# Mixer 0: the last strip's split between the first score tables, the rms root by tables, another order of the stick-breaking blocks; mixer 1: GpSimd's scaling later

## The chip, the core and the metric

The kernel runs on one core of a Trainium2 chip. The metric is the device time of one execution in microseconds; below, "us". Engines are named as in the profile: PE (TensorE), DVE (VectorE), ACT (ScalarE), POOL (GpSimd), SP (SyncE, which issues most transfers).

## The reference, cut to what matters

```python
x = LayerNorm(alpha * x + even_mixer(x))      # mixer 0: Mamba-2 SSD heads || stick-breaking heads
x = LayerNorm(alpha * x + hier_moe_0(x))
x = LayerNorm(alpha * x + odd_mixer(x))       # mixer 1: latent attention || forgetting attention
x = LayerNorm(alpha * x + hier_moe_1(x))

def _rms_norm(x, g):
    return x * rsqrt(mean(x * x, -1) + RMS_EPS) * g

# even mixer, its end
y = _ssd_scan(xs, dt, a, bs, cs) + d_skip * xs
y = _rms_norm(y * silu(z), norm_g)
# stick-breaking, per head, 256 tokens, s < t
z = q @ k.T * scale
later = reversed cumulative sum of log_sigmoid(-z) over s, without its own term
sb = where(s < t, exp(log_sigmoid(z) + later), 0) @ v
return concat([y, sb]) @ w_out

# odd mixer, both kinds of heads, per head
prob = softmax(masked logits)                 # forgetting heads add sums of log f
out = prob @ v
return concat([mla, fox]) @ w_out
```

x is [256, 1024], all values are fp32. There are 16 SSD heads and 8 stick-breaking heads of 64 in layer 0, 8 and 8 heads of 64 in layer 1.

## The kernel before, in words

Every fp32 matrix product is made of three products of two pieces: `split` (L225 to L234) takes a weight strip of 128 x 1024, copies its high piece on ACT (L232) and subtracts to get the low piece on DVE (L233). Weights come in transfers of 1 MB, in the order in which they are used, into a ring of 19 slots. There is no scheduler: every engine executes its instructions in the order in which the Python code writes them, and the code interleaves the stages by hand.

**Mixer 0.** The input projection runs through 32 strips; `presplit(i + 2)` splits two strips ahead of the strip that PE multiplies. From strip 20 on, a list `side` holds pieces of the sequence part (the SSD blocks `ssd_m` and `ssd_y`, then `sb_scores(0)` and `ssd_y(7)`), and after each strip `run_side` takes so many of them as the table `RS` says. Strips 28 to 31 are the attention's values (`v_strip`, products at L316). Behind them comes `out_proj`: 12 chunks k of the output weights, for each the three products L731, L732, L733 for two token tiles and two halves. `before(k)` runs ahead of chunk k what `PLAN0` says: `s` is `sb_scores` of a pair of heads (products L527 and L530, a mask by L293, on ACT the tables Abs, Exp, Ln at L536 to L538, on DVE L539 and the pieces L544, L545), `w` is `sb_weights` (L552, L553, the table at L555), `o` is `sb_out` (L564, L565, L566, L567), `r` is `rms` (L666), which sums squares and finds the root with shifts and Newton steps on DVE (`rsqrt_dve`, L769). The first chunks are the SSD output y (`y_scale`, L513 on ACT and L514 on DVE); the root is only applied at chunk 7. PSUM has two pools of four banks, A and B; `self.B("z")` takes the next bank of pool B and waits for its last reader.

**Mixer 1.** PE multiplies strips in the order of the list `order`: first values (`v`, L316, with norms, the turning of the latent pieces L1521 and L1522, key positions in `key_rope` and the forget gates in `forget` between them), then `q`, `kv`, and the eight strips `s`, into which the attention of the first pairs is placed (`attention(i)`): scores with row maxima on DVE (L1601, L1602) and the exponential on ACT (L1605), `norm_probs` (L1611, then L1614 and L1615, two heads each), and the split of the next strip behind them. `forget_rows` makes the rows of summed forget gates that PE multiplies at L1596. `norms` uses `rsqrt_refine` (L217 to L223). GpSimd multiplies the residual by the layer norm's gain (L836) and adds its bias (L837) in `gain_rows`, 256 columns at a time: token tile 0 inside `key_rope`, ahead of the rope's own small operations, and tile 1 in the strips s 0 and s 1. `softplus_small` (L190 to L215) is a chain of small GpSimd operations for the forget gates.

Of the kernel before, what the change touches and what calls it, by code (L numbers as in the profile page):

```python
# [41 lines left out]
for _n, _w in [("ident", 128), ("triU", 128), ("ntriSL", 128), ("sbT", 128),  # L42
# [11 lines left out]

PLAN0 = {0: [("s", 1)], 2: [("w", 0), ("w", 1)], 3: [("r", 0), ("o", 0), ("s", 2)], 4: [("o", 1)],
         5: [("s", 3)], 6: [("w", 2)], 7: [("o", 2)], 8: [("w", 3)], 9: [("o", 3)]}

# [37 lines left out]
class Builder:  # L95
# [224 lines left out]
    def mixer0(self):  # L320
# [198 lines left out]

        def sb_scores(p):  # L520
            if not p:
# [12 lines left out]
            for i, t in enumerate(ts):  # L534
                a = self.T([128, 384], name="spz")
                sc.activation(a, t[:, :384], AF.Abs)  # L536
                sc.activation(a, a, AF.Exp, scale=-1.0)
                sc.activation(a, a, AF.Ln, bias=1.0)  # L538
                v.scalar_tensor_tensor(a, t[:, :384], 0.0, a, op0=OP.max, op1=OP.add)  # L539
                Z[2 * p + i] = (t, a)  # L540
            for i in range(2):
                t, a = Z[2 * p + i]
                hi, lo = (u[:, 2 * (p % 2) + i] for u in sph)
                v.tensor_copy(hi, a)  # L544
                v.tensor_sub(lo, a, hi.bitcast(F32))  # L545
                Z[2 * p + i] = (t, a, hi, lo)
# [31 lines left out]
        for i in range(32):  # L578
# [53 lines left out]
            if i == 20:  # L632
# [4 lines left out]
                for j in range(8):  # L637
                    side += [(ssd_m, (2 * j,)), (ssd_m, (2 * j + 1,))]
                    if j:
                        side.append((ssd_y, (j - 1,)))  # L640
                side += [(sb_scores, (0,)), (ssd_y, (7,))]
            if i == 30:
# [20 lines left out]
        nc.gpsimd.dma_start(self.xres, self.a["x"])  # L663
        rr = self.S([128, 2, 8], name="rr")

        def rms(_):  # L666
            sp = self.B("ssp")
            for t in range(2):
                pe.matmul(sp[:, t:t + 1], ssq[:, 128 * t:128 * t + 128], self.one, start=True, stop=True)
            for t in range(2):  # L670
                v.tensor_scalar(rr[:, t, 1:2], sp[:, t:t + 1], 1.0 / 1024.0, RMS_EPS, op0=OP.mult, op1=OP.add)
                self.rsqrt_dve(rr[:, t, 0:1], rr[:, t, 1:2], rr[:, t, 2:])

# [15 lines left out]
        def between(k, a, t):  # L689
            if k == 7:  # L690
                sc.activation(a, a, AF.Copy, scale=rr[:, t, 0:1])

# [74 lines left out]


    def rsqrt_dve(self, y, x, t):  # L769


        v = self.nc.vector
        yi = y.bitcast(I32)
        v.tensor_scalar(yi, x.bitcast(I32), 1, None, op0=OP.arith_shift_right)
        v.tensor_scalar(yi, yi, -1.0, 1597463007.0 - 3 * 2.0 ** 23 - 2.0 ** 31, op0=OP.mult, op1=OP.add)
        for k, f in enumerate((64.0, 16.0, 4.0)):
            v.tensor_scalar(t[:, k:k + 1], x, f, None, op0=OP.mult)
        for k in range(3):
            v.scalar_tensor_tensor(t[:, 3:4], y, y, t[:, k:k + 1], op0=OP.mult, op1=OP.mult)
            v.scalar_tensor_tensor(y, t[:, 3:4], -3.0, y, op0=OP.add, op1=OP.mult)  # L780

# [603 lines left out]
    def mixer1(self, s0, moe):  # L1385
# [100 lines left out]
        def key_rope():  # L1486
            nc.gpsimd.memset(krep[:, :, :64], 0.0)
            gb.append(self.ln_rows(s0 + 4))
            for k in range(4):
                self.gain_rows(0, gb[0], slice(256 * k, 256 * k + 256))  # L1490
            self.rope(nc.gpsimd, krep[:, :, 64:80], krep[:, :, 80:96], rest[:, :, 128:144], rest[:, :, 144:160],
# [18 lines left out]
        def forget_rows():  # L1510
            fr = A["fr"]
            lp = self.B("lp")
            pe.matmul(lp[:, :128], fr[:, 0, :], self.cv("ntriSL"), start=True, stop=True)
# [147 lines left out]
        for n in range(len(order)):  # L1661
# [39 lines left out]
            if c == "s":  # L1701
                if i < 2:
                    for k in (2 * i, 2 * i + 1):
                        self.gain_rows(1, gb[0], slice(256 * k, 256 * k + 256))
                if i == 7:
# [152 lines left out]
```

## Time and profile before

| | us |
|---|---|
| median of 3 runs | 504.05 |
| lowest, highest run | 504.04, 505.17 |
| the profiled execution, its own time | 505.15 |
| its span on the profile | 503.4 |

| engine | busy us | share of the span | instructions |
|---|---|---|---|
| PE | 486.5 | 97% | 3805 |
| DVE | 301.6 | 60% | 698 |
| ACT | 246.7 | 49% | 512 |
| POOL | 74.6 | 15% | 121 |

The profile records when each instruction began and how long it took, and ends an engine's idle time with the instruction that released it. Its times below count from the start of the span. The profiled execution took 505.15, 1.1 above the median of the runs. PE's granted clock averaged 0.995 of full speed over the span.

### The profile page before, as it was taken

To read this page: it belongs to the slowest core of one execution; us is meant where nothing else is said; L and a number is where in the kernel's file an instruction comes from. 1 tells how busy PE (TensorE), PEld (TensorE's weight loads), DVE (VectorE), ACT (ScalarE), POOL (GpSimd) and SP (SyncE) were. 2 spreads that over 40 slices of the span, in tenths; PEclk is the share of its full clock that TensorE was granted. 3 is DMA by queue.
4 is the path that set the end of the run, shared out by engine and by line. 5 is a ranking of instruction groups with operands and counts; after the bars stand their busy time and mean duration, and the time that the engine had idled before them with its cause. 6 is when DMAs were issued, how large, how long until landed. Compare 5 with 4: busy or idle time off the path is not lost. (4 is left out here: it accounts for less than half of the span.)

```text
span 503.4 us, 9615 instructions
## 1 busy us (share of the span) xinstructions
PE 486.5 (97%) x3805; PEld 315.5 (63%) x3805; DVE 301.6 (60%) x698; ACT 246.7 (49%) x512; POOL 74.6 (15%) x121
## 2 busy tenths in 40 slices
PE   8999999998999999999999999999999999999992
PEld 4999998886867634352333589988777442523330
DVE  4868957767966875152305786788677761411136
ACT  3788576667774434160303667556644351612031
POOL 0074000110000000070000097400000000520003
PEclk9999999999999999999999999999999999999998
DMA  8999952005348969999999792370578799999932
GB/s 313 419 421 416 422 204 85 0 1 201 135 133 332 417 241 425 419 423 420 421 418 415 300 421 103 154 251 1 169 250 317 292 423 422 422 420 421 416 133 83
DMA packets 21313, 146.97 MB, mean 292 GB/s; under 512 B 2385, under 2 KB 2641, under 8 KB 4113
## 3 DMA queue, kind: packets, MB, share of 16 engines
q1 hardware_dynamic: 20016, 140.16, 69.2%
q0 software_dynamic: 816, 5.51, 2.9%
q8 instruction: 31, 0.51, 0.4%
q10 hardware_dynamic: 432, 0.66, 0.4%
q14 instruction: 18, 0.14, 0.1%
HBM read 145.26 MB, written 1.05 MB: 291 GB/s over the span
## 5 line engine op out<-in xcount | busy, mean ns | idle before, releaser
L1095 PE MATMUL gu<-w,XT 128*32 128x512 f32 x960 | 106.5, 593 | 0.4 <-PEq L1320 0.4
L233 DVE TENSOR_TENSOR pair<-w,pair 128x1024 fp32r<-128x1024 f32 x58 | 71.1, 1230 | 17.2 <-ACT pair L232 16.6
L1095 PEld LDWEIGHTS gu<-w,XT 128*32 128x32 f32 x960 | 30.9, 110 | 67.0 <-issue 64.5
L232 ACT ACTIVATE pair<-w 128x1024 fp32r<-128x1024 f32 x58 | 61.3, 1059 | 7.4 <-PE qu L1542 2.8
L1125 PE MATMUL dn<-w,hT 128*32 128x512 f32 x512 | 57.4, 594 | 0.0
L1105 DVE TENSOR_TENSOR hd<-sg,gu 128x256 f32<-128x256 f32 x16 | 6.7, 420 | 69.1 <-ACT sg L1103 69.0
L1148 DVE SCALAR_TENSOR_TENSOR pair<-dn,ws,pair 128x512 fp32r<-128x512 f32 x28 | 21.0, 751 | 41.0 <-ACT pair L1142 39.1
L1103 ACT ACTIVATE sg<-gu 128x256 f32<-128x256 f32 x16 | 6.2, 385 | 78.4 <-PE gu L1095 78.3
L241 PE MATMUL ps<-xh,pair 128*128 128x256 f32 x288 | 41.5, 287 | 0.3 <-ACT pair L374 0.3
L244 PE MATMUL ps<-xl,pair 128*128 128x256 f32 x288 | 39.1, 278 | 0.0
L247 PE MATMUL ps<-xh,pair 128*128 128x256 f32 x288 | 39.0, 278 | 0.0
L241 PEld LDWEIGHTS ps<-xh,pair 128*128 128x128 f32 x288 | 36.1, 189 | 2.1 <-ACT pair L374 0.8
L1125 PEld LDWEIGHTS dn<-w,hT 128*32 128x32 f32 x512 | 15.4, 110 | 33.8 <-issue 29.8
L244 PEld LDWEIGHTS ps<-xl,pair 128*128 128x128 f32 x288 | 35.8, 188 | 0.0
L247 PEld LDWEIGHTS ps<-xh,pair 128*128 128x128 f32 x288 | 35.8, 188 | 0.0
L1142 ACT ACTIVATE pair<-dn,ws 128x512 fp32r<-128x512 f32 x28 | 19.3, 688 | 29.5 <-PE dn L1125 26.8
L1060 ACT ACTIVATE XT<-gp,pp 128x256 f32<-128x256 f32 x40 | 19.2, 564 | 17.8 <-PE gp L1053 17.7
L836 POOL TENSOR_TENSOR xres<-xres,w 128x256 f32<-128x256 f32 (+1 forms) x12 | 15.9, 1322 | 79.9 <-DVE rows L1041 79.9
L1605 ACT ACTIVATE pw<-z,sm 128x128 f32<-128x128 f32 (+1 forms) x32 | 13.1, 420 | 17.8 <-DVE sm L1602 17.8
L316 PE MATMUL vp<-pair,xh 128*128 128x256 f32 x128 | 20.0, 289 | 1.8 <-DVE pair L233 1.6
L316 PEld LDWEIGHTS vp<-pair,xh 128*128 128x128 f32 x128 | 16.7, 188 | 3.1 <-DVE pair L233 2.0
L431 DVE SCALAR_TENSOR_TENSOR cy<-ps,pp,cy 128x255 f32<-128x255 f32 (+2 forms) x36 | 17.3, 480 | 2.0 <-ACT cy L428 1.1
(378 smaller groups left out, 902.3 us busy)
## 6 DMA issues: line engine op xcount, KB each, us to landing
w<-in_wgu_dram SPq DMA_DIRECT2D x60, 1024.0 KB, 11.6
w<-in_wd_dram SPq DMA_DIRECT2D x32, 1024.0 KB, 13.3
w<-in_w_dram SPq DMA_DIRECT2D x15, 1024.0 KB, 18.4
w<-in_wout_dram SPq DMA_DIRECT2D x10, 1024.0 KB, 17.5
wh<-in_wgu_dram POOLq DMA_DIRECT2D x4, 1024.0 KB, 7.3
w<-in_ln_dram SPq DMA_DIRECT2D x4, 1024.0 KB, 13.8
w<-in_wfox_dram SPq DMA_DIRECT2D x4, 1024.0 KB, 8.8
w<-in_wfv_dram SPq DMA_DIRECT2D x2, 1024.0 KB, 18.9
```

Source lines behind the costliest of these rows:

```text
L232: self.nc.scalar.activation(vh, src, AF.Copy)
L233: (self.nc.gpsimd if pool else self.nc.vector).tensor_tensor(vl, src, vh.bitcast(F32), op=OP.subtract)
L241: mm(ps, hi[:, c, :], xh[:, c, :], start=(c == 0), stop=False)
L244: mm(ps, hi[:, c, :], xl[:, c, :], start=False, stop=False)
L247: mm(ps, lo[:, c, :], xh[:, c, :], start=False, stop=(c == n - 1))
L316: mm(o, xx[:, 4 * k + c, 128 * t:128 * t + 128], ww[:, c, :], start=(k == 0 and n == 0), stop=(k == 1 and n == 11))
L431: v.scalar_tensor_tensor(y[:, k:], ps[:, :256 - k], self.pp[:, i:i + 1], y[:, k:], op0=OP.mult, op1=OP.add)
L1060: sc.activation(xt[:, c, :], b[:, i], AF.Identity, bias=bb, scale=g)
L1095: pe.matmul(gu[t][32 * e:32 * e + 32, :], XT[t][:, c, o:o + 32], w[:, e, :], start=(c == 0), stop=(c == 7))
L1125: pe.matmul(b[32 * e:32 * e + 32, :], ht[:, k, 32 * e:32 * e + 32], w[:, e, :], start=(k == 0), stop=(k == 1))
L1142: sc.activation(y, dn[t, s], AF.Copy, scale=WS[t][:, q:q + 1])
L1148: v.scalar_tensor_tensor(yl, b, WS[t][:, q:q + 1], yh.bitcast(F32), op0=OP.mult, op1=OP.subtract)
```

## The change

It does four things.

1. In mixer 0 `sb_scores` takes a function `mid` that it calls after the first head's tables; for the first pair this is `presplit(31)`, the split of the last strip.
2. The root of the rms norm is found with ACT's Ln and Exp and one Newton step (`rsqrt_refine`, a chunk later) for both token tiles at once; `rsqrt_dve` is gone.
3. `PLAN0` moves the outputs of pair 1 from chunk 4 to chunk 3, and the weights of pair 2 from chunk 6 to chunk 5, ahead of the scores of pair 3.
4. In mixer 1 `key_rope` no longer scales the residual. `gain_rows` runs for both tiles in the strips s 0 to s 3. The PSUM tile `lp` of `forget_rows` comes from pool A.

```diff
--- before.py
+++ after.py
@@ -52,8 +52,8 @@
 RS = [3, 4, 3, 1, 4, 3, 0, 4, 2, 3, 1, 1]
 LP = (6, 7)
 
-PLAN0 = {0: [("s", 1)], 2: [("w", 0), ("w", 1)], 3: [("r", 0), ("o", 0), ("s", 2)], 4: [("o", 1)],
-         5: [("s", 3)], 6: [("w", 2)], 7: [("o", 2)], 8: [("w", 3)], 9: [("o", 3)]}
+PLAN0 = {0: [("s", 1)], 2: [("w", 0), ("w", 1)], 3: [("r", 0), ("o", 0), ("o", 1), ("s", 2)], 4: [("r", 1)],
+         5: [("w", 2), ("s", 3)], 7: [("o", 2)], 8: [("w", 3)], 9: [("o", 3)]}
 
 
 def constants():
@@ -517,7 +517,8 @@
 
         sph = []
 
-        def sb_scores(p):
+        def sb_scores(p, mid=None):
+
             if not p:
                 sph.extend(self.G([128, 4, 384], F32R, name="sph") for _ in range(2))
 
@@ -538,6 +539,8 @@
                 sc.activation(a, a, AF.Ln, bias=1.0)
                 v.scalar_tensor_tensor(a, t[:, :384], 0.0, a, op0=OP.max, op1=OP.add)
                 Z[2 * p + i] = (t, a)
+                if mid and not i:
+                    mid()
             for i in range(2):
                 t, a = Z[2 * p + i]
                 hi, lo = (u[:, 2 * (p % 2) + i] for u in sph)
@@ -638,7 +641,7 @@
                     side += [(ssd_m, (2 * j,)), (ssd_m, (2 * j + 1,))]
                     if j:
                         side.append((ssd_y, (j - 1,)))
-                side += [(sb_scores, (0,)), (ssd_y, (7,))]
+                side += [(sb_scores, (0, lambda: presplit(31))), (ssd_y, (7,))]
             if i == 30:
                 wsplit = self.out_split(12, LEAD0, 16)
                 wsplit(0)
@@ -661,15 +664,18 @@
         yl = self.G([128, 8, 256], F32R, name="yl")
         self.xres = self.G([128, 2, 1024], name="xres")
         nc.gpsimd.dma_start(self.xres, self.a["x"])
-        rr = self.S([128, 2, 8], name="rr")
-
-        def rms(_):
+        rr = self.S([128, 8], name="rr")
+
+        def rms(step):
+
+            if step:
+                return self.rsqrt_refine(rr[:, 0:2], rr[:, 2:4], rr[:, 4:6])
             sp = self.B("ssp")
             for t in range(2):
                 pe.matmul(sp[:, t:t + 1], ssq[:, 128 * t:128 * t + 128], self.one, start=True, stop=True)
-            for t in range(2):
-                v.tensor_scalar(rr[:, t, 1:2], sp[:, t:t + 1], 1.0 / 1024.0, RMS_EPS, op0=OP.mult, op1=OP.add)
-                self.rsqrt_dve(rr[:, t, 0:1], rr[:, t, 1:2], rr[:, t, 2:])
+            v.tensor_scalar(rr[:, 2:4], sp[:, :2], 1.0 / 1024.0, RMS_EPS, op0=OP.mult, op1=OP.add)
+            sc.activation(rr[:, 6:8], rr[:, 2:4], AF.Ln)
+            sc.activation(rr[:, 0:2], rr[:, 6:8], AF.Exp, scale=-0.5)
 
         plan = PLAN0
 
@@ -688,7 +694,7 @@
 
         def between(k, a, t):
             if k == 7:
-                sc.activation(a, a, AF.Copy, scale=rr[:, t, 0:1])
+                sc.activation(a, a, AF.Copy, scale=rr[:, t:t + 1])
 
         return self.out_proj(12, LEAD0, wsplit, mix, 1, 3, before, between, early=8)
 
@@ -765,19 +771,6 @@
                 self.gdone(tiles)
             yield acc
 
-
-    def rsqrt_dve(self, y, x, t):
-
-
-        v = self.nc.vector
-        yi = y.bitcast(I32)
-        v.tensor_scalar(yi, x.bitcast(I32), 1, None, op0=OP.arith_shift_right)
-        v.tensor_scalar(yi, yi, -1.0, 1597463007.0 - 3 * 2.0 ** 23 - 2.0 ** 31, op0=OP.mult, op1=OP.add)
-        for k, f in enumerate((64.0, 16.0, 4.0)):
-            v.tensor_scalar(t[:, k:k + 1], x, f, None, op0=OP.mult)
-        for k in range(3):
-            v.scalar_tensor_tensor(t[:, 3:4], y, y, t[:, k:k + 1], op0=OP.mult, op1=OP.mult)
-            v.scalar_tensor_tensor(y, t[:, 3:4], -3.0, y, op0=OP.add, op1=OP.mult)
 
     def residual_half(self, t, s, acc, stats=True):
 
@@ -1486,8 +1479,6 @@
         def key_rope():
             nc.gpsimd.memset(krep[:, :, :64], 0.0)
             gb.append(self.ln_rows(s0 + 4))
-            for k in range(4):
-                self.gain_rows(0, gb[0], slice(256 * k, 256 * k + 256))
             self.rope(nc.gpsimd, krep[:, :, 64:80], krep[:, :, 80:96], rest[:, :, 128:144], rest[:, :, 144:160],
                       self.cv("cosk").rearrange("p (t n) -> p t n", t=2),
                       self.cv("sink").rearrange("p (t n) -> p t n", t=2), [128, 2, 16])
@@ -1509,7 +1500,7 @@
 
         def forget_rows():
             fr = A["fr"]
-            lp = self.B("lp")
+            lp = self.A("lp")
             pe.matmul(lp[:, :128], fr[:, 0, :], self.cv("ntriSL"), start=True, stop=True)
             pe.matmul(lp[:, 128:256], fr[:, 1, :], self.cv("triU"), start=True, stop=True)
             self.row_pieces(frow[:, 128:384], lp)
@@ -1699,9 +1690,9 @@
                 mix[0] = self.G([128, 8, 256], F32R, name="mixm")
                 mix[1] = self.G([128, 8, 256], F32R, name="mixf")
             if c == "s":
-                if i < 2:
+                if i < 4:
                     for k in (2 * i, 2 * i + 1):
-                        self.gain_rows(1, gb[0], slice(256 * k, 256 * k + 256))
+                        self.gain_rows(k // 4, gb[0], slice(256 * (k % 4), 256 * (k % 4) + 256))
                 if i == 7:
                     finish(*pend)
                     pend = None
```

Three places in the instructions' order, each as it was and as it is now. Names are the program's: `pair` and `w` are pieces and weights, `spz` and `sph` the scores' tables and pieces, `xsT` the SSD output.

The first is DVE in mixer 0, around the first scores. Before:

```order
L496 TENSOR_TENSOR xsT<-xsT,z 128x256
L539 SCALAR_TENSOR_TENSOR spz<-z,spz 128x384 x2
L544 CAST sph<-spz 128x384
L545 TENSOR_TENSOR sph<-spz,sph 128x384
L544 CAST sph<-spz 128x384
L545 TENSOR_TENSOR sph<-spz,sph 128x384
L233 TENSOR_TENSOR pair<-w,pair 128x1024
L495 SCALAR_TENSOR_TENSOR xsT<-xsT,pp,yo 128x256
```

Now:

```order
L496 TENSOR_TENSOR xsT<-xsT,z 128x256
L540 SCALAR_TENSOR_TENSOR spz<-z,spz 128x384
L233 TENSOR_TENSOR pair<-w,pair 128x1024
L540 SCALAR_TENSOR_TENSOR spz<-z,spz 128x384
L547 CAST sph<-spz 128x384
L548 TENSOR_TENSOR sph<-spz,sph 128x384
L547 CAST sph<-spz 128x384
L548 TENSOR_TENSOR sph<-spz,sph 128x384
L495 SCALAR_TENSOR_TENSOR xsT<-xsT,pp,yo 128x256
```

The subtraction L233 of strip 31 moved from behind both heads' pieces to between their tables; L495, the last SSD block, follows the pieces directly. ACT's copy L232 moved in the same way.

The second is PE around the scores of pair 3. `acc` are the output projection's sums, `msb` is the mask. Before:

```order
L293 MATMUL z<-msb,identb 128x2x128
L731 MATMUL acc<-pair,yh 128x512
L732 MATMUL acc<-pair,yl 128x512
L733 MATMUL acc<-pair,yh 128x512
L731 MATMUL acc<-pair,yh 128x512
L732 MATMUL acc<-pair,yl 128x512
L733 MATMUL acc<-pair,yh 128x512
L552 MATMUL z<-sph,sbT 128x384 x2
L553 MATMUL z<-spz,one 128x128
L552 MATMUL z<-sph,sbT 128x384 x2
L553 MATMUL z<-spz,one 128x128
```

Now:

```order
L739 MATMUL acc<-pair,yh 128x512
L555 MATMUL z<-sph,sbT 128x384 x2
L556 MATMUL z<-spz,one 128x128
L555 MATMUL z<-sph,sbT 128x384 x2
L556 MATMUL z<-spz,one 128x128
L528 MATMUL z<-qk 128x256 x2
L531 MATMUL z<-qk 128x128 x2
L293 LDWEIGHTS identb
L293 MATMUL z<-msb,identb 128x2x128
```

The weights of pair 2 (L552 before, L555 now) moved from behind the scores of pair 3 and one chunk's half to directly ahead of those scores.

The third is POOL at the start of mixer 1. `krep` are the rotated keys, `rest` what the norms leave. Before:

```order
L1487 MEMSET krep 128x2x64
L836 TENSOR_TENSOR xres<-xres,w 128x256
L837 TENSOR_TENSOR xres<-xres,w 128x256
L836 TENSOR_TENSOR xres<-xres,w 128x256
L837 TENSOR_TENSOR xres<-xres,w 128x256
L836 TENSOR_TENSOR xres<-xres,w 128x256
L837 TENSOR_TENSOR xres<-xres,w 128x256
L836 TENSOR_TENSOR xres<-xres,w 128x256
L837 TENSOR_TENSOR xres<-xres,w 128x256
L1378 TENSOR_TENSOR rt<-rest,cc 128x32
```

Now:

```order
L1480 MEMSET krep 128x2x64
L1371 TENSOR_TENSOR rt<-rest,cc 128x32
L1372 TENSOR_TENSOR rt<-rest,cc 128x32
L1373 TENSOR_TENSOR rt<-rest,cc 128x32
L1374 TENSOR_TENSOR rt<-rest,cc 128x32
```

The eight scaling operations are gone from ahead of the rope. They stand behind the forget gates' last copies (L1506, now L1497), ahead of the eight that stood there before, so that sixteen follow each other, with the two transfers of MoE weights (L162) behind them.

## Rows read from the trace of the kernel before

**Rows 1.** PE's waits: line waited for, us in total, times, longest us.

```profile
PE vp L316 <- DVE pair L233: 1.6, 2, 1.3
```

**Rows 2.** Timeline, end of mixer 0's strips: start, us, engine, line, operation [idle before].

```profile
112.55 1.05 ACT L232 ACTIVATE pair<-w 128x1024 fp32r<-128x1024 f32 x1
...
114.87 1.22 DVE L233 TENSOR_TENSOR pair<-w,pair 128x1024 fp32r<-128x1024 f32 x1
...
116.97 0.42 ACT L501 ACTIVATE sq<-xsT 128x256 f32<-128x256 f32 x1 [3.38 <-DVE xsT L496]
...
120.05 0.50 PE L732 MATMUL acc<-pair,y 128*128 128x512 f32 x1 [0.34 <-DVE y L514]
```

**Rows 3.** Timeline, chunks 3 to 7 of mixer 0's output projection.

```profile
131.26 0.15 DVE L671 TENSOR_SCALAR rr<-ssp 128x1 f32<-128x1 f32 x1
...
131.69 0.70 PE L527 MATMUL z<-qk 64*128 64x256 f32 x4
...
132.54 0.39 PE L293 MATMUL z<-msb,identb 128*128 128x256 bf16 x2
...
139.40 1.27 PE L527 MATMUL z<-qk 64*128 64x256 f32 x3
...
141.04 0.39 PE L293 MATMUL z<-msb,identb 128*128 128x256 bf16 x2
...
141.36 0.49 ACT L536 ACTIVATE spz<-z 128x384 f32<-128x384 f32 x1 [2.43 <-PE z L293]
...
142.66 0.51 PE L552 MATMUL z<-sph,sbT 128*128 128x384 f32 x2
...
143.72 0.48 PE L731 MATMUL acc<-pair,yh 128*128 128x512 f32 x1
...
147.96 0.51 PE L733 MATMUL acc<-pair,yh 128*128 128x512 f32 x1 [0.22 <-DVE pair L233]
```

**Rows 4.** Timeline of DVE, start of mixer 1.

```profile
289.76 0.74 DVE L220 TENSOR_TENSOR mt<-ss 128x2 f32<-128x2 f32 x1 [0.56 <-ACT ss L1439]
290.54 0.65 DVE L221 TENSOR_TENSOR mt<-mt,ms 128x2 f32<-128x2 f32 x1
...
294.43 1.75 DVE L233 TENSOR_TENSOR pair<-w,pair 128x1024 fp32r<-128x1024 f32 x1
...
297.11 0.16 DVE L220 TENSOR_TENSOR mt<-ss 128x2 f32<-128x2 f32 x1 [0.56 <-ACT ss L1439]
```

**Rows 5.** Timeline of PE, the same stretch and the one behind it.

```profile
292.17 1.10 PE L316 MATMUL vp<-pair,xh 128*128 128x256 f32 x8
...
298.44 0.44 PE L1521 MATMUL ct<-cc,cn 128*128 128x128 f32 x2
...
301.31 1.10 PE L316 MATMUL vp<-pair,xh 128*128 128x256 f32 x8
302.25 0.63 PE L316 MATMUL vp<-pair,xl 128*128 128x256 f32 x4
```

**Rows 6.** Timeline of POOL, first and last of tile 1's eight scaling operations.

```profile
314.86 0.74 POOL L836 TENSOR_TENSOR xres<-xres,w 128x256 f32<-128x256 f32 x1
...
320.19 0.73 POOL L837 TENSOR_TENSOR xres<-xres,w 128x256 f32<-128x256 f32 x1
```

**Rows 7.** DVE's timeline, first two strips' normalisation; then line L1614: least/median/longest ns, first to last.

```profile
320.17 0.84 DVE L1614 TENSOR_SCALAR pw<-pw,sm 128x128 f32<-128x128 f32 x1
...
325.45 0.28 DVE L1614 TENSOR_SCALAR pw<-pw,sm 128x128 f32<-128x128 f32 x1
...
L1614 DVE TENSOR_SCALAR pw<-pw,sm x16: 274/284/837, 320.2 to 364.0; 128x128 f32<-128x128 f32 x16
```

**Rows 8.** Timeline, the forget rows and the product that reads them.

```profile
334.68 0.46 PE L1513 MATMUL lp<-cc,da 128*128 128x128 f32 x2 [0.46 <-issue]
...
338.68 0.20 DVE L1516 COPY lrow<-lrow 128x128 bf16<-128x128 bf16 x1
...
338.99 0.50 PE L1596 MATMUL z<-lrow,sel 128*128 128x384 bf16 x2
```

## The prediction

> **What bounds the kernel now.** I read the profile's busy shares first: TensorE is at work for 97% of the span, so only its few idle places and the things that set them can give or take time. Next I read TensorE's list of waits, where the largest entry is the wait for the split of a value strip on VectorE, 1.6 us in two times, the longer one 1.3 [rows 1]. That one lies at the last strip of mixer 0, where the change works. Then I read the timeline at the four places that the change touches. The reader should see that in mixer 0 VectorE splits strip 31 in the middle of the attention's first scores [rows 2] and that TensorE later runs into three short stalls around chunks 3 to 7 of the output projection [rows 3]. In mixer 1 VectorE operations take longer exactly while GpSimd scales [rows 4], and TensorE is slower there [rows 5]. GpSimd's second batch of scaling ends on the first attention strip's normalisation [rows 6, 7], and a strictly serial chain of ScalarE and VectorE leads from there to TensorE's product with the forget rows [rows 8].
>
> **Mixer 0, last strip.** Before, the strip's copy and subtraction stand behind both heads' tables: ScalarE 1.05 us at 112.55, VectorE 1.22 at 114.87 [rows 2]. Now they stand between the heads. TensorE's 1.3 us stall for strip 31 should go. But TensorE then goes straight to the output projection, whose second product (L732) already waits 0.34 for the low piece of y at 120.05 [rows 2]. That piece comes at the end of a serial chain: the casts of the second head, the SSD output of the last block (L495, L496), its square on ScalarE at 116.97, the split of the first output weight, and L514. In this chain the second head's tables are now later by ScalarE's 1.05, since the copy stands ahead of them, and the 1.22 subtraction is no longer between the casts and L495. So the chain is earlier by 1.22 - 1.05 = 0.17, and the other 1.1 of the stall only moves to L732. Bounds: 0.17 by this chain, 1.5 if it does not bind (a rival below).
>
> **Mixer 0, order of the blocks.** The weights of pair 2 now stand ahead of the scores of pair 3. That puts 143.72 - 142.66 = 1.06 us of products in front of the scores. Against this, the scores' block took 141.04 - 139.40 = 1.64 us to its first mask where the block of pair 2 took 132.54 - 131.69 = 0.85 [rows 3]: its second product needs a PSUM bank that the outputs of pair 1 have to leave, and those outputs now come a chunk earlier. So 0.79 goes. From the scores' mask, ScalarE (its L536 at 141.36 had waited 2.43 us for it), the casts and the split lead to L733 at 147.96, where TensorE waits [rows 3]. This chain is 1.06 - 0.79 = 0.27 later, less the 0.17 from above: between 0.17 earlier (if the moved blocks, side by side, save some of the 0.27) and 0.1 later. I take **-0.1 for all of mixer 0**, nearer to the end at which the first block's 0.17 is kept, and keep -0.2 to +0.1 for the range.
>
> **Mixer 0, the root.** 22 operations on one column each of 0.15 us and more, from 131.26 on [rows 3], become one operation on VectorE, two on ScalarE and four more a chunk later. VectorE has about 3 us less to do there. I cost this at nothing: the result is first read at chunk 7, and between 131.69 and 139.40 TensorE does not wait. ScalarE gets two tiny table operations; the Exp and Ln tables are the ones that the scores around them use, so no table load is added. If that cover were gone, the price would be those two operations, below 0.5 us.
>
> **Mixer 1, the scaling leaves the start.** While GpSimd scales, VectorE's tiny L220 takes 0.74 us against 0.16 in the next tile, its successor L221 0.65 right after, and the split L233 1.75 [rows 4] against 1.22 in mixer 0 [rows 2]. So VectorE stands still until a scaling operation ends, and again at the next of its operations: three times by 0.58, 0.49 and 0.53. TensorE needs 298.44 - 292.17 = 6.27 us for 40 products and one turn (L1521 twice, L1522). A later undisturbed stretch of eight products takes 302.25 - 301.31 = 0.94, so 40 take 4.70; with 0.25 for the turn and 0.1 for a restart behind it (estimates, below the 0.44 that two products of a turn last by their row) that is about 5.07 [rows 5]. **-1.2** for TensorE and for all that follows it.
>
> **Mixer 1, the scaling arrives later.** GpSimd's operations come at 320.19 - 314.86 = 5.33 for seven, 0.76 each [rows 6]. The forget computation ahead of them shifts with VectorE and ScalarE, so the sixteen start near 314.86 - 1.2 = 313.7 and last 16 x 0.76 = 12.2 us, to 325.9. The normalisation of the first strip starts at 320.17 - 1.2 = 319.0 and now lies wholly under them: four multiplications (L1614, L1615 twice) and the split L233 behind them. Before, one alone was caught, the very first: 0.84 against 0.28 a strip later, 0.56 too much, and it is the one outlier of sixteen (median 284 ns, longest 837) [rows 7]. For each of the five I take the mean of the four holds seen, (0.58 + 0.49 + 0.53 + 0.56) / 4 = 0.54, together 2.70. The 0.56 of before is part of the old time: **+2.14**. Does it reach the end? ScalarE and VectorE alternate strip by strip, each waiting for the other, up to the copy of the forget rows at 338.68, and TensorE's L1596 starts at 338.99, just behind it [rows 8]. So the chain, now 2.14 - 1.2 = 0.9 late, sets TensorE there, and TensorE's earlier arrival is waited away. Bounds: three holds of 0.49 (1.47) or five of a whole 0.73 us operation [rows 6] (3.65).
>
> The Trainium skill, "SBUF — State Buffer", section "Who interferes with whom", speaks against this move: whoever issues first holds the port pair that VectorE and GpSimd share for the whole instruction, and the other is blocked fully. It names tensor_scalar among the operations that can take the pair and tensor_tensor with two SBUF inputs among those that contend. The traced holds of 0.49 to 0.58 are parts of a 0.73 us operation; by the Trainium skill alone, five whole operations could be lost, and the sum would be +1.8.
>
> **The rest.** Tile 0's scaled residual is read only at the residual of mixer 1, behind all of this. GpSimd's two weight transfers are issued behind the sixteen operations instead of eight, some 5 us later; their reader is the MoE behind the output projection. The new PSUM pool of `lp` removes a wait of 0.46 on TensorE at 334.68 [rows 8]; TensorE then waits longer at L1596, whose other input arrives at 338.88 by the same rows. At most 0.1, taken as 0.
>
> **Sum:** -0.1 - 1.2 + 2.14 = **+0.84 us**. The profiled execution took 505.15, so it would take 506.0; that execution is the slowest of three, and from the median of 504.05 the same sum gives **504.9**. Its own range goes with the bounds: 1.47 - 0.56 - 1.2 - 0.2 = -0.5 (503.6) to 3.65 - 0.56 - 1.2 + 0.1 = +2.0 (506.0).
>
> **Rivals.**
> *VectorE gets through.* Of sixteen L1614 only one was ever caught, and L1614 and L1615 are of another kind (one SBUF tensor and a column) than L220, L221 and L233. If only operations with two tensors are held, or VectorE's closely spaced operations keep their turn, the moved scaling costs nothing: -0.56 - 1.2 - 0.1 = -1.9, 502.2; with one hold left, 502.7. Against it: the one that was caught had 0.84, and it began within 0.02 us of a scaling operation.
> *Slower: the scaling reaches the second strip.* If each held operation waits for a whole scaling operation, five are 3.65 us and VectorE in turn holds GpSimd back for its own durations, over 2 us in all, so that the last scaling operation ends near 328. The second strip's normalisation would come at 325.45 [rows 7] - 1.2 + 3.1 = 327.3 and lose one more: 6 x 0.73 = 4.38, less 0.56, 1.2 and 0.1 is +2.5, 506.6. It decides if the last scaling operation ends behind that second normalisation's start. By the order alone it comes out at 325.9, so it needs the full holds.
> *Mixer 0 keeps its stall's worth.* If y's low piece is earlier by all of the strip's stall, mixer 0 gives 1.5 in place of 0.1: +0.84 - 1.4 = -0.6, 503.5. For it: TensorE's 1.3 us wait is real. Against it: L732 waits already.
>
> **Chances.** Forecast 0.43, VectorE gets through 0.25, second strip 0.16, mixer 0 0.16. About 0.3% (1.5 us) is what a measurement of this kernel can tell from no change: 502.5 to 505.6. Faster: most of the first rival and a little of the third together with it, 0.22. Slower: the second rival and the upper end of the forecast's range, 0.23. The rest, 0.55, is the same. The range runs from 502.1 (the first rival) to 506.4 (most of the way to the second), leaving out under 2 in 10.
>
> **What would show it.** In the profile after: no TensorE wait for L233 at strip 31, and one of 1 us or more at the second product of the output projection instead; L220 at 0.16 in both tiles and about 5.1 us for the 40 products; the scaling operations in a row from about 313.7 to 326; the first strip's four multiplications at 0.7 to 1.0 us and its split at 1.7; TensorE waiting some 2 us at the product with the forget rows. The multiplications at 0.28 and 0.34 would make the prediction wrong by the first rival; long ones in the second strip too by the second; no wait at the output projection's start by the third.

## The result, and the profile after

The changed kernel takes **507.39 us** (median of four runs, 507.37 to 507.71) against 504.15 for the kernel before, measured with it: 3.24 us slower, ratio 1.006 with a 95% interval of 1.0047 to 1.0072. The forecast of 504.9 and its range up to 506.4 were too low.

PE's list of waits in the changed kernel (line waited for, us in total, times, longest us):

```profile
PE acc L739 <- DVE pair L233: 1.8, 1, 1.8
...
PE acc L737 <- ACT y L513: 1.0, 1, 1.0
...
PE acc L738 <- DVE y L514: 0.8, 1, 0.8
...
PE acc L737 <- ACT pair L232: 0.5, 1, 0.5
```

The wait of [rows 1] at strip 31 is gone. In its place stand 1.0 and 0.8 at the head of the output projection, and at chunk 7 there is a new wait of 1.8 behind one of 0.5. Now the timeline of PE at the places that answer to [rows 2, 3, 5, 8]:

```profile
31.25 0.59 PE L465 MATMUL cbp<-bc 128*128 128x256 f32 x2
...
117.83 0.50 PE L737 MATMUL acc<-pair,y 128*128 128x512 f32 x1 [1.01 <-ACT y L513]
...
119.09 0.79 PE L738 MATMUL acc<-pair,y 128*128 128x512 f32 x1 [0.76 <-DVE y L514]
...
122.61 0.40 PE L737 MATMUL acc<-pair,y 128*128 128x512 f32 x1
...
148.65 0.50 PE L739 MATMUL acc<-pair,yh 128*128 128x512 f32 x1 [1.77 <-DVE pair L233]
...
152.94 0.55 PE L737 MATMUL acc<-wb,sbh 128*128 128x512 f32 x1
...
294.40 1.10 PE L316 MATMUL vp<-pair,xh 128*128 128x256 f32 x8
...
299.45 0.38 PE L1512 MATMUL ct<-cc,cn 128*128 128x128 f32 x2
...
341.57 0.50 PE L1587 MATMUL z<-lrow,sel 128*128 128x384 bf16 x2 [0.79 <-DVE lrow L1507]
```

Three rows of the kernel before are needed beside those shown already, from the same view:

```profile
32.00 0.60 PE L465 MATMUL cbp<-bc 128*128 128x256 f32 x2
...
122.00 0.39 PE L731 MATMUL acc<-pair,y 128*128 128x512 f32 x1
...
150.85 0.40 PE L731 MATMUL acc<-wb,sbh 128*128 128x512 f32 x1
```

The first pair of rows lies in code that the change does not touch, and there the profiled execution of before is 0.75 late. That is part of why it took 505.15 where its median is 504.05. The last column below takes it out.

| the same product | before | after | difference | + 0.75 |
|---|---|---|---|---|
| L465, untouched code | 32.00 | 31.25 | -0.75 | 0.00 |
| first product with y's low piece | 120.05 | 119.09 | -0.96 | -0.21 |
| tenth product of the projection | 122.00 | 122.61 | +0.61 | +1.36 |
| chunk 7, the product that waits for the split | 147.96 | 148.65 | +0.69 | +1.44 |
| first product on the borrowed buffer (`wb`) | 150.85 | 152.94 | +2.09 | +2.84 |
| second turn of mixer 1 | 298.44 | 299.45 | +1.01 | +1.76 |
| product with the forget rows | 338.99 | 341.57 | +2.58 | +3.33 |

So mixer 0 lost 2.8 us in two jumps of some 1.5, mixer 1's start gave back 1.1, and from there to the forget rows 1.6 were lost. Each jump lies behind a long wait, and the granted clock shows why. The stretches of the changed kernel (columns: stretch, its length, busy us and instructions of PE, PEld (TensorE's weight loads), DVE, ACT and POOL, then the granted clock, DMA share and GB/s):

```profile
116.00:118.00 2.00, 0.99 (x10) 0.59 (x6) 0.59 (x1) 1.98 (x4) 1.22 (x2) 1.00 0.45 78
118.00:120.00 2.00, 1.25 (x3) 0.84 (x4) 2.00 (x4) 2.00 (x5) 0.00 (x0) 0.78 0.99 418
120.00:122.00 2.00, 2.00 (x6) 1.51 (x6) 1.00 (x2) 1.94 (x6) 0.00 (x0) 0.50 1.00 369
...
146.00:148.00 2.00, 0.73 (x2) 0.30 (x2) 1.93 (x5) 1.31 (x3) 0.00 (x0) 1.00 0.79 332
148.00:150.00 2.00, 1.35 (x6) 1.18 (x7) 2.00 (x3) 0.78 (x2) 0.00 (x0) 0.96 0.37 53
150.00:152.00 2.00, 2.00 (x9) 1.99 (x8) 0.53 (x2) 1.99 (x4) 0.00 (x0) 0.50 0.75 299
```

Behind each wait TensorE runs for some 3 us at the lower of its two levels, 1.2 instead of 2.4 GHz, and six products fit into 2 us where before had nine. The same stretches of before:

```profile
120.00:122.00 2.00, 1.95 (x9) 1.61 (x9) 1.96 (x3) 1.97 (x6) 0.00 (x0) 1.00 0.88 369
...
150.00:152.00 2.00, 2.00 (x11) 1.65 (x10) 1.13 (x1) 2.00 (x4) 0.00 (x0) 1.00 1.01 414
```

In before the clock is 1.00 throughout both places, although its waits there (0.2, 1.3 and 0.3; later 0.5 and 0.2) add up to as much at the first place. There 1.2 us of work lie between the first two and over 3 between the 1.3 and the 0.3.

The two places of mixer 1 in the changed kernel, VectorE and GpSimd with the first and last of the sixteen scaling operations:

```profile
316.63 0.73 POOL L829 TENSOR_TENSOR xres<-xres,w 128x256 f32<-128x256 f32 x1
...
329.24 1.79 POOL L830 TENSOR_TENSOR xres<-xres,w 128x256 f32<-128x256 f32 x1
```

```profile
321.15 0.79 DVE L1605 TENSOR_SCALAR pw<-pw,sm 128x128 f32<-128x128 f32 x1
321.86 0.34 DVE L1606 TENSOR_SCALAR pw<-pw,sm 128x256 f32<-128x256 f32 x1
322.12 0.74 DVE L1605 TENSOR_SCALAR pw<-pw,sm 128x128 f32<-128x128 f32 x1
322.79 0.83 DVE L1606 TENSOR_SCALAR pw<-pw,sm 128x256 f32<-128x256 f32 x1
323.54 1.21 DVE L233 TENSOR_TENSOR pair<-w,pair 128x1024 fp32r<-128x1024 f32 x1
...
327.81 0.75 DVE L1605 TENSOR_SCALAR pw<-pw,sm 128x128 f32<-128x128 f32 x1
328.49 0.82 DVE L1606 TENSOR_SCALAR pw<-pw,sm 128x256 f32<-128x256 f32 x1
```

Three multiplications of the first strip are held (0.51, 0.46, 0.49 over the undisturbed 0.28 and 0.34), one gets through, and so does the split. In the second strip two more are held (0.47, 0.48). One row of ScalarE in mixer 1 has no counterpart in before: a pause of 2.22 us for which the profile names nothing ("issue").

```profile
302.82 0.37 ACT L1517 ACTIVATE cu<-ct,pp 128x128 f32<-128x128 f32 x1 [2.22 <-issue]
```

### The profile page after: what moved, and what is told of

It reads as the page before. It is cut to its first block, busy times and chain, and to the rows that moved or that the text cites. A ratio compares the mean times of both kernels' runs of the same rounds, so it can differ in the third digit from the quotient of the medians.

```text
span 505.9 us, 9598 instructions
## 1 busy us (share of the span) xinstructions
PE 487.0 (96%) x3805; PEld 317.0 (63%) x3805; DVE 298.9 (59%) x679; ACT 247.3 (49%) x514; POOL 73.6 (15%) x121
## 5 line engine op out<-in xcount | busy, mean ns | idle before, releaser
L233 DVE TENSOR_TENSOR pair<-w,pair 128x1024 fp32r<-128x1024 f32 x58 | 70.7, 1223 | 17.1 <-ACT pair L232 16.9
L232 ACT ACTIVATE pair<-w 128x1024 fp32r<-128x1024 f32 x58 | 61.3, 1059 | 5.9 <-PE qu L1533 2.6
L829 POOL TENSOR_TENSOR xres<-xres,w 128x256 f32<-128x256 f32 (+1 forms) x12 | 15.3, 1278 | 79.9 <-DVE rows L1034 79.9
L830 POOL TENSOR_TENSOR xres<-xres,w 128x256 f32<-128x256 f32 (+1 forms) x12 | 17.8, 1479 | 0.9
```

The lines of the kernel that those rows point to most:

```text
L232: self.nc.scalar.activation(vh, src, AF.Copy)
L233: (self.nc.gpsimd if pool else self.nc.vector).tensor_tensor(vl, src, vh.bitcast(F32), op=OP.subtract)
L830: g.tensor_tensor(r, r, gb[:, 1, cs], op=OP.add)
```

## The experiments

The theory after the result: the loss is the clock that falls behind two waits in mixer 0. The rival: the scaling moved into the attention strips. Medians, and 0.1 us means little: the runs of a kernel with a fall of the clock spread over up to 3.8 us (the changed kernel's four over only 0.3), those of the others over 0.6 to 1.8.

| kernel | median us | before beside it | ratio, 95% interval |
|---|---|---|---|
| m0_only | 507.27 | 504.47 | 1.0053, 1.0035 to 1.0070 |
| m1_only | 504.25 | 504.47 | 0.9996, 0.9988 to 1.0005 |
| mid_only | 504.91 | 504.47 | 1.0005, 0.9994 to 1.0016 |
| plan_only | 506.82 | 504.47 | 1.0037, 1.0022 to 1.0052 |
| after_fill | 505.13 | 504.50 | 1.0007, 0.9998 to 1.0016 |
| rms_only | 506.63 | 504.50 | 1.0035, 1.0024 to 1.0046 |
| m0_w0 | 503.41 | 504.50 | 0.9977, 0.9966 to 0.9987 |
| m1_mid | 502.99 | 504.50 | 0.9968, 0.9956 to 0.9980 |
| act2 | 505.75 | 504.31 | 1.0029, 1.0018 to 1.0041 |
| rms_pad | 512.56 | 504.31 | 1.0158, 1.0145 to 1.0171 |
| after_oldroot | 508.18 | 504.31 | 1.0071, 1.0058 to 1.0084 |
| both_new | 501.52 | 504.31 | 0.9946, 0.9933 to 0.9959 |

**The halves.** m0_only has points 1 to 3 of the change, m1_only its point 4.

> Mixer 0 of the changed kernel (strip 31 between the heads, root by tables, new order of the blocks), mixer 1 as before. Theory 1 (the loss is TensorE's clock: two waits in mixer 0's output projection let the granted clock fall to half, twice): +3.0 us against the kernel before, two stretches of some 3 us at 0.5 behind L737/L738 and behind L739 of chunk 7. Rival (the loss is the scaling that runs into the first attention strips of mixer 1): about -0.1 us, and any lower clock without weight.

> Mixer 0 as before, mixer 1 of the changed kernel (scaling behind the forget gates, lp from pool A). Theory 1: -1.4 us at the start of mixer 1, +1.8 at the forget rows, together +0.4 us, no stretch at a lower clock. Rival (the scaling is the loss): +3 us.

Measured: +2.80 and -0.22. The loss is in mixer 0, and the scaling is not it. In m1_only four operations are held instead of the five above (by 0.37 to 0.49, the last of them in the second strip), and the clock is 1.00 until TensorE's last product. The forecast for it was +0.4. Two of its products, the second turn of mixer 1 and the product with the forget rows:

```profile
296.31 0.38 PE L1519 MATMUL ct<-cc,cn 128*128 128x128 f32 x2
...
337.81 0.50 PE L1594 MATMUL z<-lrow,sel 128*128 128x384 bf16 x2 [0.81 <-DVE lrow L1514]
```

They lie 41.50 apart, against 338.99 - 298.44 = 40.55 in before: the scaling on the strips costs 0.95 there.

**One part at a time.** mid_only and plan_only.

```diff
-                side += [(sb_scores, (0,)), (ssd_y, (7,))]
+                side += [(sb_scores, (0, lambda: presplit(31))), (ssd_y, (7,))]
```

> Before with one edit, the split of strip 31 between the two heads' tables. Theory 1: the two waits at the head of the output projection join to one of about 1.8 us, the clock falls to 0.5 behind it, and the second wait (chunk 7) stays in two parts at the full clock: +1.4 us at chunk 1, of which some is absorbed by waits up to chunk 7, so +0.8 to +1.4 at the end. Rival (the fall of the clock comes from something else in the new mixer 0): -0.2 us and full clock.

```diff
-PLAN0 = {..., 3: [("r", 0), ("o", 0), ("s", 2)], 4: [("o", 1)], 5: [("s", 3)], 6: [("w", 2)], ...
+PLAN0 = {..., 3: [("r", 0), ("o", 0), ("o", 1), ("s", 2)], 5: [("w", 2), ("s", 3)], ...
```

> Before with one edit, the order of the blocks (outputs of pair 1 at chunk 3, weights of pair 2 at chunk 5 ahead of the scores of pair 3), root as before. Theory 1: the waits for the weights' table and for the split of chunk 7 join to one at L733 of some 1.5 us or more, and the clock falls behind it: +1 to +1.6 us. Rival (the second fall follows only from the first, which makes ScalarE's and VectorE's chain late): one wait under 0.8 us, full clock, within 0.3 us of before.

The stretches of mid_only, then of plan_only:

```profile
116.00:120.00 4.00, 2.23 (x14) 1.43 (x11) 2.57 (x5) 3.85 (x7) 1.23 (x2) 0.99 0.63 236
120.00:124.00 4.00, 4.00 (x12) 3.10 (x12) 2.07 (x4) 3.87 (x9) 0.00 (x0) 0.59 0.98 317
...
148.00:152.00 4.00, 3.79 (x19) 3.01 (x19) 2.52 (x4) 2.98 (x6) 0.00 (x0) 1.00 0.60 182
```

```profile
120.00:124.00 4.00, 4.00 (x20) 3.30 (x19) 2.06 (x4) 3.87 (x9) 0.00 (x0) 1.00 1.02 430
...
148.00:152.00 4.00, 3.85 (x14) 3.51 (x15) 2.51 (x4) 3.25 (x6) 0.00 (x0) 0.67 0.75 244
```

In these executions each part makes its own fall: the split the first, the order the second, without the other. The medians are +0.44 for mid_only, below the +0.8 to +1.4 that was expected and not clear of noise, and +2.35 for plan_only, above its +1 to +1.6. The mean granted clock, which is on record for every run, suggests why mid_only's twelve runs spread so far. It is 0.991 or 0.992 in five of them (505.46 to 506.52) and 0.994 or 0.995 in the other seven (503.86 to 504.96, median 504.13, which is -0.34). In plan_only it is 0.989 or 0.991 in four runs (506.82 to 507.86) and 0.995 in three (505.47 to 505.94, median +1.23). m0_only falls into three groups: 0.993 and 0.994 (505.34 and 505.86), 0.990 and 0.991 (506.75 to 507.85), 0.988 (509.05 to 509.16). The profiled executions, whose falls were seen, are in the group with the lowest clock each time, and some 3 us at half take 0.003 off the mean (an estimate from the stretches above). So the fall most likely comes in some runs of a kernel and not in others, and is worth about 1.6 us where it comes. This is a sign and no proof: the mean also has the idle end of the span in it, and in before it varies from 0.992 to 0.996 without a fall in mixer 0 in the execution that was profiled.

plan_only has a price without a fall too, since the order costs something more when the root is the long one: the scores of pair 2 now need the PSUM bank of the sums of squares, which VectorE leaves late.

```profile
131.59 0.70 PE L527 MATMUL z<-qk 64*128 64x256 f32 x2
132.56 0.48 PE L527 MATMUL z<-qk 64*128 64x256 f32 x1 [0.27 <-DVE rr L671]
...
133.41 0.39 PE L293 MATMUL z<-msb,identb 128*128 128x256 bf16 x2
```

From the block's start to its first mask that is 1.82 us in plan_only against 0.85 in [rows 3], 0.97 more.

**The waits kept, the clock held.** after_fill adds products that nobody reads.

```diff
+            n = {(0, 0, 0, 0): 6, (0, 0, 0, 1): 4, (7, 0, 0, 2): 11}.get((k, t, s, part), 0)
+            if n:
+                b = acc[1][1] if not k else self.B("fill")
+                for _ in range(n):
+                    pe.matmul(b[:, :384], self.sbT, sph[0][:, 0], start=True, stop=True, skip_group_check=True)
```

> The changed kernel with filler products in its two long waits of mixer 0: ten products of 384 columns ahead of and behind the first L737, eleven ahead of L739 of chunk 7, into PSUM that nothing reads. They add work to TensorE and shorten no chain. Theory 1 (the price of the two waits is the clock that falls behind them): the granted clock stays at 1.00 through both places, and the time is 2 to 3 us below the changed kernel's (504.5 to 505.5). Rival (the waits themselves are the price, or something else lowers the clock): 507.4 or more, since products are added.

The stretches of after_fill, then the two products that had waited and the first product on the borrowed buffer:

```profile
118.00:120.00 2.00, 1.94 (x9) 1.30 (x9) 2.00 (x4) 2.00 (x4) 0.00 (x0) 1.00 1.00 422
120.00:122.00 2.00, 2.00 (x10) 1.61 (x10) 1.14 (x2) 1.94 (x5) 0.00 (x0) 1.00 0.93 324
...
150.00:152.00 2.00, 2.00 (x12) 1.35 (x12) 1.32 (x2) 1.87 (x4) 0.00 (x0) 1.00 1.01 406
```

```profile
119.23 0.50 PE L749 MATMUL acc<-pair,y 128*128 128x512 f32 x1
...
147.29 0.50 PE L752 MATMUL acc<-pair,yh 128*128 128x512 f32 x1
...
150.18 0.40 PE L746 MATMUL acc<-wb,sbh 128*128 128x512 f32 x1
```

The product with y's low piece starts at the same place as in the changed kernel (119.23 against 119.09), so the chain is no shorter. The clock stays at 1.00, chunk 7's product comes 1.4 us earlier, and the time is 505.13: +0.63 to before (not clear of noise) where the changed kernel has +3.24, with 21 products more. Its L465 starts at 31.36, so by the measure of the table above the first product on the borrowed buffer comes at 150.18 + 0.64 = 150.82, against 150.85 in before and 2.84 later in the changed kernel. This is the experiment that shows the cause: the price of the two waits is the clock behind them.

**The chain made shorter.** m0_w0 is mid_only with the copy of the first output weight ahead of the last SSD block on ScalarE.

```diff
+                def last_y():
+                    src = self.ring[16][:, :1024]
+                    hi, lo = self.pair()
+                    sc.activation(hi, src, AF.Copy)
+                    ssd_y(7)
+                    v.tensor_tensor(lo, src, hi.bitcast(F32), op=OP.subtract)
+                    wsplit(99)[0] = (hi, lo)
```

> Before with two edits in mixer 0: strip 31 split between the heads, and the first output weight's copy on ScalarE ahead of the last SSD block instead of behind its square, so that the chain to y's pieces is about 1 us shorter. Theory 1: TensorE's wait at the head of the output projection falls from 1.8 us to some 0.5 us, the clock stays at 1.00, and 1.2 to 1.5 us of before's waits go: 503 us. Rival (any split amid the scores lowers the clock): as with the split alone, 505 us.

PE's timeline of m0_w0 at the head of the projection:

```profile
116.95 0.49 PE L740 MATMUL acc<-pair,y 128*128 128x512 f32 x1
...
118.11 0.50 PE L741 MATMUL acc<-pair,y 128*128 128x512 f32 x1 [0.67 <-DVE y L514]
```

One long wait, of 0.67, is left, the clock is 1.00 in all stretches there, and the kernel is 1.1 us faster than before. The same split that lowers the clock in mid_only gains here.

**The scaling elsewhere.** m1_mid runs all sixteen operations ahead of the long part of the forget gates. The lines that it adds (it takes both old places out):

```diff
+            if (c, i) == ("v", 2):
+                for k in range(8):
+                    self.gain_rows(k // 4, gb[0], slice(256 * (k % 4), 256 * (k % 4) + 256))
```

> Before with the sixteen scaling operations of mixer 1 in the middle of the forget gates' computation (behind L203, ahead of L206), so that they run from about 300 to 313 and none is left when the first attention strip is normalised. Theory 1 (GpSimd holds VectorE's operations where they stand on the chain): -1.4 us at the start, the 0.56 of before in the first strip gone, small holds by the forget gates' tiny operations: -1.2 to -1.9 us. Rival (the scaling costs the same wherever it runs): within 0.4 us of before.

GpSimd's first and last scaling operation in m1_mid, and the first strip's first multiplication:

```profile
300.61 0.74 POOL L836 TENSOR_TENSOR xres<-xres,w 128x256 f32<-128x256 f32 x1
...
315.83 0.74 POOL L837 TENSOR_TENSOR xres<-xres,w 128x256 f32<-128x256 f32 x1
```

```profile
318.03 0.29 DVE L1612 TENSOR_SCALAR pw<-pw,sm 128x128 f32<-128x128 f32 x1
```

Measured -1.51. The same work costs next to nothing where VectorE has slack, and about 1.3 more in m1_only, where it stands on the strips' chain.

**The root.** rms_only has the new root in the old order.

> Before with one edit, the root by two tables and one Newton step a chunk later. Every theory here expects no difference (within 0.3 us): nothing waits for VectorE there. If ScalarE's two operations or a table load delayed the scores' tables, +0.3 us or more and a longer wait at chunk 7.

Measured +2.13, a plain miss, and without a fall of the clock. Its timeline shows two prices: PE waits for a PSUM bank that VectorE frees behind the refinement, and ScalarE pauses in mixer 1.

```profile
140.01 0.48 PE L528 MATMUL z<-qk 64*128 64x256 f32 x1 [0.76 <-DVE sbh L570]
...
302.44 0.53 ACT L1521 ACTIVATE cthl<-cu 128x384 fp32r<-128x384 f32 x1 [1.68 <-issue]
```

The second stands 160 us behind the edit, in code that the edit doesn't touch. The pause shows in each of the six kernels with two more ScalarE instructions (the changed kernel, m0_only, after_fill, rms_only, and the two below) and in none of the others. act2 and rms_pad ask whether the root matters for it or the count. act2 is before with two operations that nobody reads:

```diff
+            sc.activation(dm[:, 0:2], self.one[:, 0:1].to_broadcast([128, 2]), AF.Ln)
+            sc.activation(dm[:, 2:4], dm[:, 0:2], AF.Exp, scale=-0.5)
```

> Before with nothing changed but two tiny table operations (Ln and Exp of two columns) that nobody reads, on ScalarE where the changed kernel has its root. Theory A (the pause of 1.3 to 2.2 us on ScalarE in mixer 1 comes with two instructions more on its stream, whatever they compute): ScalarE pauses by 1 us or more for nothing the profile shows near the turning of the latent pieces, and the time is 0.5 to 1.2 us over before. Theory B (the pause belongs to the root by tables, by its readers or its tables' values): no pause, within 0.3 us of before.

rms_pad is rms_only with twelve more at the start of mixer 1:

```diff
+            if t:
+                dm = self.S([128, 16], name="dm")
+                for k in range(12):
+                    sc.activation(dm[:, k:k + 1], self.one, AF.Copy)
```

> The root by tables alone, and twelve tiny copies that nobody reads on ScalarE in mixer 1, just ahead of an operation for which ScalarE waits over 4 us anyway. Theory A (the pause sits at a fixed count of instructions on ScalarE): with twelve more it moves twelve instructions up the program, into that wait, and shows no more; the time falls to the root's other price in mixer 0, 0.5 to 1.0 us over before. Theory B: the pause stays at the turning of the latent pieces, and the time stays 2 us over before.

ScalarE in act2, then in rms_pad:

```profile
301.98 0.37 ACT L1529 ACTIVATE cu<-ct,pp 128x128 f32<-128x128 f32 x1 [1.45 <-issue]
```

```profile
292.22 1.22 ACT L1431 ACTIVATE dm<-one 128x1 f32<-128x1 f32 x12
302.56 0.20 ACT L1435 ACTIVATE ss<-ms 128x2 f32<-128x2 f32 x1 [9.12 <-issue]
```

Two idle instructions bring the pause by themselves (act2, +1.44, above the expected +0.5 to +1.2), so it belongs to the count, not to the root. With twelve more it begins earlier in the program, as theory A said, but it is not hidden, and the time missed both theories: +8.25. Of the 9.12 us some 3 are the wait for VectorE that was there anyway, to 296.6; the other 6 are the pause. TensorE waits 6.1 us behind it and loses its clock too.

The traces say more. In all six kernels the pause stands behind the 382nd instruction of ScalarE that the trace records. And the trace lists DMA packets one by one, those that carry instructions among them (kind "instruction" on the page, here queue q14, 8 KB each). One of them ends shortly before the end of every pause:

| kernel | instruction packet ends | ScalarE goes on | later by |
|---|---|---|---|
| changed kernel | 301.40 | 302.82 | 1.42 |
| m0_only | 304.06 | 305.36 | 1.30 |
| after_fill | 297.83 | 299.14 | 1.31 |
| rms_only | 301.13 | 302.44 | 1.31 |
| act2 | 300.58 | 301.98 | 1.40 |
| rms_pad | 301.25 | 302.56 | 1.31 |

The pause's end moves by 6 us from kernel to kernel and keeps its distance to this packet. So ScalarE waits there for its next instructions. The kernels without the two instructions have such a packet too (it ends at 301.00 in before) and do not stop at that place; why they do not is not shown.

**The old root in the changed kernel.**

> The changed kernel with the root of before (22 operations on VectorE). By theory A no pause on ScalarE in mixer 1, so GpSimd's forget gates end about 1 us earlier against TensorE and the scaling holds four operations of the attention strips instead of five: 0.3 to 0.8 us below the changed kernel, 506.6 to 507.1; both falls of the clock in mixer 0 stay, the second with a wait up to 0.5 us longer as VectorE does the long root. Rival (the root is without weight here): 507.4.

Measured 508.18, +3.87 to before where the changed kernel has +3.24. The intervals overlap, so it is not shown to be slower, but the 0.3 to 0.8 that it was to gain did not come. The part on mixer 1 held: no pause, and four multiplications held instead of five. What was left out is plan_only's second price, found above: in the new order the long root delays the scores of pair 2 (1.52 from the block's start to its mask, against 0.86 in the changed kernel), and both falls of the clock stay. The new root and the new order cost more alone (+2.13 and +2.35) than together with the split (m0_only, +2.80).

**Both repairs.** both_new is m0_w0 with m1_mid's edit.

> Before with the two edits that gained by themselves: mixer 0's last strip between the heads with the first output weight's copy ahead of the last SSD block, and mixer 1's scaling in the middle of the forget gates. They touch different stretches, so the gains should add: -1.1 - 1.5 = -2.6 us, 501.9. Rival (a gain of mixer 0 is waited away later): -1.5 us.

Measured 501.52, 2.79 us under before, and so some 6 under the changed kernel, which lies 3.24 above it. The two gains alone are 1.09 + 1.51 = 2.60: they add.

## Why the prediction was wrong, point by point

- **Last strip: the chain right, its price wrong.** L732 was to come 0.17 earlier and came 0.21 earlier. The step that failed is the sentence that the other 1.1 us of the stall "only moves to L732". Moved there (1.01 of it to the product just ahead), it joined the wait that was there already, TensorE stood still for most of 2 us, and the clock fell: +1.57 between two rows of the table that lie eight products apart. The third rival (PE keeps the 1.5) did not happen; its "against", that L732 waits already, was the start of the right thought.
- **Order of the blocks: the same.** The chain to chunk 7 was to move by -0.17 to +0.1. In after_fill, where the clock stays up, its product comes 147.96 - 147.29 = 0.67 earlier than in the profiled execution of before, of which 32.00 - 31.36 = 0.64 are there already at L465: 0.03 earlier, as forecast. What failed is that three short waits (0.5, 0.2 and a bank) became one of 1.8 right behind one of 0.5 and cost the clock again, 2.84 - 1.44 = 1.40. For all of mixer 0 the sum had -0.1; it measured +2.84 with the two falls and -0.03 in after_fill without them.
- **The root: costed at nothing, wrong.** The prediction asked who reads the result, and overlooked that the scores wait for PSUM banks which VectorE frees behind the root: 0.76 in rms_only. The second price, ScalarE's pause in mixer 1, was in no row of before. In the changed kernel the first is gone, since with the new order the scores of pair 3 reach their mask in 0.85. For the second, compare the time from the second turn to the forget rows with m1_only's 41.50, where no pause is: 42.12 in the changed kernel, so the pause of 2.22 costs some 0.6; 338.25 - 296.68 = 41.57 in after_fill, where a pause of 1.31 costs next to nothing. (The old root is 24 operations by the trace, not 22, which changes nothing.)
- **Mixer 1's start: right.** The 40 products and the turn take 299.45 - 294.40 = 5.05 where 5.07 was forecast and before had 6.27, so -1.22 for a forecast of -1.2; 2.84 - 1.76 = 1.1 by the rows of the table. L220 takes 0.16 in both tiles.
- **The scaling on the strips: right in kind, too high in size.** Five holds of 0.54 were forecast, five of 0.46 to 0.51 came, three in the first strip and two in the second; the split got through, and beside it a GpSimd operation took 1.80 instead of 0.73. +2.14 was forecast, +1.57 came by the table with the pause's part in it, and +0.95 in m1_only, where no pause is: four holds of 0.37 to 0.49, together 1.79, less the 0.56 of before, and not all of the rest reached the forget rows. So this term was too high by 1.2, and mixer 1 as a whole, +0.94 in the sum, came to -0.22 alone. The second rival had the reach into the second strip right, in m1_only too, and the size of the holds wrong. Whole operations of 0.73, as the rule of the Trainium skill's "SBUF — State Buffer", section "Who interferes with whom", would allow at most, were not lost: the trace agrees that one engine holds the other, and five of the strips' ten operations got through.
- **Sum.** Forecast +0.84; with 2.94 more in mixer 0 and about 0.5 less in mixer 1 it is the +3.33 of the table. No rival had the clock, and so the range missed. That the error of mixer 1 went the other way hid a part of it; this was luck.

## What to carry to other kernels

A wait is not only its own length. Before moving idle time along TensorE's path, look at which waits it will join: several short ones with over 1 us of work between them kept the clock at 1.00 here, the same time with 0.5 to 0.7 between the pieces cost nearly as much again at 0.50 behind it, and by the mean clock on record not in every run. Shorten the chain that ends the wait first, then remove the wait ahead of it, as m0_w0 did; and put GpSimd's operations on SBUF where VectorE has slack, not merely "later".

## What the runs showed of the hardware that was not expected

- Waits of 1.0 and 0.8 with 0.5 of work between them, or of 0.5 and 1.8 with 0.7 between, let the granted clock fall from 1.00 to 0.50 for about 3 us in the profiled executions; before's waits of 0.2, 1.3 and 0.3, with 1.2 and over 3 us of work between them, and m0_w0's one of 0.67 did not.
- Two ScalarE instructions more in mixer 0 bring a pause of 1.3 to 2.2 us on ScalarE in mixer 1, fourteen more one of some 6. In all six kernels it stands behind the 382nd recorded instruction and ends 1.30 to 1.42 us after an instruction packet has arrived. The DMA engines are full there: act2 moves 410 GB/s from 300 to 302. That the packet is late because weights are queued ahead of it is only argued: no run had the weights' transfers moved.
- VectorE's multiplications and GpSimd's operations do not alternate strictly. Of ten VectorE operations in the two strips five were held, each by 0.46 to 0.51, less than the 0.73 of one GpSimd operation; and beside each split a GpSimd operation took 1.8.
